# Projections made two chunks at a time: sixteen wide products, then sixteen narrow ones

## The chip, the cores and the metric

The kernel runs on one core of one Trainium2 chip. The metric is device time in microseconds (us): the time of one execution of the program. Lower is better. The parts of the core that matter here are TensorE (PE in the profile), which multiplies matrices and leaves its sums in PSUM banks; ScalarE (ACT) and VectorE (DVE), which prepare operands and empty those banks; SyncE (SP), which issues the loads of the weights; and GpSimd (POOL), which does little.

## The reference

The reference is an encoder of two layers on an input of 256 tokens with 1024 channels, all in float32. Each layer adds two sub-layers to the stream `h`:

```
u, q, k, v, g_pool, g_attn = split(rmsnorm(x) @ w_in)     # 1024, 3 x 1536, 1024, 1024 columns
pooled  = centred means of u (windows 2, 4, 8, 16 for 4 groups of 256) - u
pool    = (pooled_g @ w_pool_g for each group) * pool_scale
attn    = dilated window attention, 12 heads of 128 in 3 groups of 4,
          with relative-position bias, the groups combined by their softmax sums
merged  = sigmoid(g_pool) * (pool @ w_a) + sigmoid(g_attn) * (attn @ w_b)
x      += merged @ w_o
a, g    = split(rmsnorm(x) @ w_up)                        # 2816 columns each
x      += (gelu(conv3(a) + conv_b) * g) @ w_down
```

A final RMSNorm follows. Nearly all the work is in the products with `w_in`, `w_pool`, `w_a`, `w_b`, `w_o`, `w_up` and `w_down`.

## The kernel before, in words

**How a product keeps its precision.** A float32 matrix is held as two parts, a high one and a low one, in the type fp32r. A weight piece (mostly 1024 input rows by 128 output columns) arrives by a DMA as `raw` (L117); ACT casts it to the high part `wh` (L177), and DVE subtracts that from `raw` to make the low part `wl` (L178). Here this is called a split. The activations are held the same way, side by side: `x2` is [high | low], 256 tokens each, 512 columns wide. A product then has two kinds of step. A wide one multiplies `wh` by all 512 columns of [high | low]; a narrow one multiplies `wl` by the 256 high columns, and adds into the second half of the same bank. The product low by low is left out.

**A projection.** One chunk of 128 output channels is made by `proj` (L489): it takes a weight piece from `W.get`, claims one of the four PSUM banks of the pool `mmp`, and calls `two_sums` (L473), which issues the steps: eight wide (one for each 128 rows of the 1024) and eight narrow. The flag `turns["rest"]` turns over at each call. If one call does the wide steps first, the next does the narrow ones first. So PE's stream is eight wide, then sixteen narrow (eight of this chunk and eight of the next), then sixteen wide, and so on. The chunk is then read by ACT and DVE (an eviction), mostly in `add_up` (L508): ACT copies one half, DVE adds the other to it. Only after that does the bank come free.

**The callers.** In each layer these use `two_sums`:

- the pooling inputs `u` (L811): 8 chunks, one after another; in layer 0 one step of `build_bias` (L367) goes ahead of each, five in all, which puts a pair of small products (`f_ps`, L374) in PE's stream;
- the queries and keys (L962): six groups `PAIRS` of two query chunks and two key chunks, 24 chunks. In the second group (`m == 1`) one step of `pool_out` goes ahead of each of the four chunks;
- `pool_out` (L841): each step makes two chunks of the pooled output, with only two wide and two narrow steps for each (the groups have 256 channels). Below, such a step is called a pool pair, 1 to 4. ACT and DVE scale both (L855 and the line after) and split the result into `po2`;
- from the fourth group on (`m >= 3`), after every second chunk, one step of the attention: scores (`s_ps`, L882), turning (`pt_ps`, L911) or weighing (`o_ps`), on PE's fp32 and fp32r products;
- `pa` (L987): 8 chunks of `po2 @ w_a`, most of them followed by an attention step;
- the gates (L995): 16 chunks, 8 for the pooled branch and then 4 and 4 for the attention branch, each 4 followed by four chunks `b_ps` of `at2 @ w_b`, with four wide and four narrow steps each (L1012);
- the MLP (L1085): for each of 22 blocks `f` a chunk `g` and, from `f = 4` on, a chunk `a`. From `f = 6` on, after every two blocks, two rows of the product with `w_down` follow (`residual_mm`, L512 to L514), three products for each output tile.

The values `v`, the products with `w_o` and `w_down` and the first four `a` chunks are made in other ways and do not use `two_sums`.

**What sets the order.** The program is written in one order, and each engine works through its own queue in that order. Work that depends on another engine's waits for it by semaphores, which the tile framework places. Splits are asked for three pieces ahead (`LOOK = 3`); there are three `raw` buffers and five pairs of `wh` and `wl` (`RAW` and `BUFS`, L84). `W.get` issues the splits that are due before the products that use the piece, so on ACT and DVE they stand between the evictions of earlier chunks. PSUM has eight banks: four in `mmp`, four in `acc` (sums of `residual_mm`, scores and others).

Of the kernel before, what the change touches and what calls it, by code (L numbers as in the profile page):

```python
# [10 lines left out]
F32 = mybir.dt.float32  # L11
# [5 lines left out]
P = 128  # L17
D = 1024
S = 256
# [185 lines left out]
def encoder(ctx, tc, x, w_in, w_pool, pool_scale, w_a, w_b, w_o, norm1, norm2, w_up, conv_w,  # L205
# [264 lines left out]

    turns = {"rest": False}

    def two_sums(ps, wh, wl, x2, nk):  # L473

        steps = [(k, True) for k in range(nk)]
        rests = [(k, False) for k in range(nk)]  # L480
        steps = rests + steps if turns["rest"] else steps + rests
        for n, (k, wide) in enumerate(steps):
            out, w, x = (ps, wh, x2[:, k]) if wide else (ps[:, 1], wl, x2[:, k, 0])
            nc.tensor.matmul(  # L484
                out, w(k), x, start=(n == 0), stop=(n == 2 * nk - 1), skip_group_check=turns["rest"]
            )
        turns["rest"] = not turns["rest"]

    def proj(x2):  # L489

        i, (wh, wl) = W.get()
        ps = mmp.tile([P, 2, S], F32, tag="mm", name="proj_ps")
        two_sums(ps, lambda k: wh[:, k, :], lambda k: wl[:, k, :], x2, KD)
        W.free(i)
        return ps[:, 0], ps[:, 1]

    def halves(a):

# [2 lines left out]
    def in_order(a):  # L501

        return a.rearrange("p (m t) -> p t m", t=2)
# [248 lines left out]
    for l in range(DEPTH):  # L752
# [50 lines left out]
        for gi in range(3, -1, -1):  # L803
            w = WINDOWS[gi]
            u = sm.tile([P, 2, S + 2 * PAD], F32, tag="u", name="u")
            nc.vector.memset(u[:, :, 0:PAD], 0.0)
            nc.vector.memset(u[:, :, PAD + S :], 0.0)
            for j in range(2):
                if l == 0:
                    next(bias, None)  # L810
                add_up(in_order(u[:, j, PAD : PAD + S]), [halves(a) for a in proj(x2)])  # L811
            cur, n = u, S + 2 * PAD
            sh = 1
            while sh < w:
                nxt = sm.tile([P, 2, S + 2 * PAD], F32, tag="us", name="us")
                n -= sh
                nc.vector.tensor_add(
                    out=nxt[:, :, 0:n], in0=cur[:, :, 0:n], in1=cur[:, :, sh : sh + n]
                )
                cur = nxt  # L820
                sh *= 2
            hw = w // 2
            o = PAD - hw
            e = edge[:, gi, 0:hw].unsqueeze(1).to_broadcast([P, 2, hw])
            nc.vector.tensor_mul(out=cur[:, :, o : o + hw], in0=cur[:, :, o : o + hw], in1=e)
            if hw > 1:
                e = edge[:, gi, hw : w - 1].unsqueeze(1).to_broadcast([P, 2, hw - 1])
                r = slice(o + S - hw + 1, o + S)
                nc.vector.tensor_mul(out=cur[:, :, r], in0=cur[:, :, r], in1=e)
            pd = sm.tile([P, 2, S], F32, tag="us", name="pd")  # L830
            nc.vector.scalar_tensor_tensor(
                out=pd, in0=cur[:, :, o : o + S], scalar=1.0 / w, in1=u[:, :, PAD : PAD + S],
                op0=ALU.mult, op1=ALU.subtract,
            )
            both = pl2[gi // 2][:, gi % 2 * 2 : gi % 2 * 2 + 2]
            ph, pl = both[:, :, 0], both[:, :, 1]
            pd = pd.rearrange("p k (m t) -> p k t m", t=2)
            nc.scalar.copy(out=ph, in_=pd)
            nc.vector.tensor_sub(out=pl, in0=pd, in1=ph.bitcast(F32))
            pooled[gi] = both  # L840
        def pool_out(po2):  # L841
            for j in range(2):
                i, (wh, wl) = W.get()
                for gg in range(2):
                    for oc in range(2):
                        ps = mmp.tile([P, 2, S], F32, tag="mm", name="pool_ps")
                        cc = slice(oc * P, (oc + 1) * P)
                        two_sums(
                            ps, lambda k: wh[:, 2 * gg + k, cc], lambda k: wl[:, 2 * gg + k, cc],
                            pooled[2 * j + gg], 2,  # L850
                        )
                        c = 4 * j + 2 * gg + oc
                        sc = hps[:, l, c : c + 1]
                        po = sm.tile([P, 2, P], F32, tag="u", name="po")
                        nc.scalar.mul(out=po, in_=halves(ps[:, 1]), mul=sc)  # L855
                        nc.vector.scalar_tensor_tensor(
                            out=po, in0=halves(ps[:, 0]), scalar=sc, in1=po, op0=ALU.mult, op1=ALU.add
                        )
                        nc.scalar.copy(out=po2[:, c, 0], in_=po)
                        nc.vector.tensor_sub(out=po2[:, c, 1], in0=po, in1=po2[:, c, 0].bitcast(F32))  # L860
                    if gg:
                        W.free(i)
                    yield
# [87 lines left out]
        for m, c in enumerate(PAIRS):  # L951
            if m == 1:
                po2 = two_parts("m2", "po2")
                pool_parts = pool_out(po2)
            if m == 2:

                qkl = big.tile([P, 2, HPG, 2, P], F32R, tag="xn", name="qkl")
                ql, kl = qkl[:, 0], qkl[:, 1]
            for n in range(4):
                if m == 1:  # L960
                    next(pool_parts)
                src, rest = (halves(a) for a in proj(x2))  # L962
                hd = 2 * c + n % 2
                scale = HD**-0.5 if n < 2 else 1.0
                if hd < HPG:
                    hi, lo = ((qh, ql) if n < 2 else (kh, kl))
                    nc.scalar.mul(out=hi[:, hd], in_=src, mul=scale)
                    nc.vector.scalar_tensor_tensor(
                        out=lo[:, hd], in0=src, scalar=scale, in1=hi[:, hd].bitcast(F32),
                        op0=ALU.mult, op1=ALU.subtract,  # L970
                    )
                    nc.vector.scalar_tensor_tensor(
                        out=lo[:, hd], in0=rest, scalar=scale, in1=lo[:, hd].bitcast(F32),
                        op0=ALU.mult, op1=ALU.add,
                    )
                else:
                    o = (q if n < 2 else kk)[:, hd - HPG]
                    nc.scalar.mul(out=o, in_=rest, mul=scale)
                    nc.vector.scalar_tensor_tensor(
                        out=o, in0=src, scalar=scale, in1=o, op0=ALU.mult, op1=ALU.add  # L980
                    )
                if m >= 3 and n % 2:
                    step()
# [10 lines left out]

        def gate(c):  # L995
            th = gates[:, c % 4, :]
            add_up(th, proj(x2))
            nc.scalar.activation(th, th, AF.Tanh, scale=0.5)  # L998
            return th

# [7 lines left out]
        for c4 in range(2):  # L1008
            ths = [gate(4 * c4 + j) for j in range(4)]
            for j2 in range(2):  # L1010
                i, (wh, wl) = W.get()
                for j in range(2):  # L1012
                    c = 4 * c4 + 2 * j2 + j
                    ps = mmp.tile([P, 2, S], F32, tag="mm", name="b_ps")
                    cc = slice(j * P, (j + 1) * P)
                    two_sums(ps, lambda k: wh[:, k, cc], lambda k: wl[:, k, cc], at2, 4)
                    m = sm.tile([P, S], F32, tag="u", name="m")
                    add_up(m, (ps[:, 0], ps[:, 1]))
                    nc.vector.scalar_tensor_tensor(
                        out=m, in0=ths[2 * j2 + j], scalar=1.0, in1=m, op0=ALU.add, op1=ALU.mult  # L1020
                    )
                    nc.vector.tensor_add(out=m, in0=m, in1=pa[:, c, :])
                    m = halves(m)
                    nc.scalar.copy(out=mh[:, c], in_=m)
                    nc.vector.tensor_sub(out=ml[:, c], in0=m, in1=mh[:, c].bitcast(F32))
                W.free(i)
# [50 lines left out]
        for i, _ in held:  # L1077
            W.free(i)
        last = keep_entry(ps)
        g_first = [proj(x2)]  # L1080
        turn_entry(1, last)

        def up(f):
            w0, w1, w2, b = (prm[:, l, j * NF + f : j * NF + f + 1] for j in range(4))
            if f < ENTRY:  # L1085
                a = a_first[:, f, :]
            else:
                a = sm.tile([P, S], F32, tag="u", name="a")
                add_up(in_order(a), [halves(b) for b in proj(x2)])
            sums = g_first.pop() if f == 0 else proj(x2)  # L1090
            y = sm.tile([P, S], F32, tag="s", name="y")
            nc.scalar.activation(y, a, AF.Identity, bias=b, scale=w1)  # L1092
            nc.vector.scalar_tensor_tensor(  # L1093
# [85 lines left out]
```

## Time and profile before

| what | before |
| --- | --- |
| median of 3 runs | 880.12 us (879.62 to 880.17) |
| the profiled execution's own time | 880.35 us |
| its span, from the first to the last instruction | 878.6 us |
| mean granted clock of TensorE | 0.998 |
| PE busy | 870.6 us, 99% |
| DVE busy | 684.6 us, 78% |
| ACT busy | 524.3 us, 60% |
| POOL busy | 13.5 us, 2% |
| moved by DMA | 164.47 MB, 187 GB/s |

A row of the timeline gives the start and the length in us, the engine, the line of the kernel, the operation, what it writes and what it reads, the tile's shape, and how many instructions of one kind in a row were put together (x16). A length reaches from the start of the first to the end of the last. Consecutive products overlap on PE, so the time that a run of products takes is read from its start to the start of the next run. A note in brackets is the time that the engine idled ahead of the row, and what it waited for.

### The profile page before, as it was taken

The page shows a single profiled execution, that of the slowest core. Times are in us where ns is not written, and L with a number is a line of the kernel's source. Part 1 is how long each engine was busy: PE and PEld are TensorE (multiplying, and loading weights), DVE is VectorE, ACT ScalarE, POOL GpSimd, SP SyncE. Part 2 cuts the span into 40 slices and gives each one's busy share as a digit, 9 for nine tenths or more (in the row PEclk, how much of TensorE's full clock was granted, in tenths as well). Part 3 has the DMA queues.
Part 4 walks back from the last instruction along what each step waited for, and adds up shares of the span by engine and source line. Part 5 has one row for each costly group of instructions (what it writes and reads, how often), then busy time and mean ns, then how long its engine had stood idle before and what let it go on. Part 6 is the DMA issues. An engine that isn't in the chain of part 4 may idle for free.

```text
span 878.6 us, 12705 instructions
## 1 busy us (share of the span) xinstructions
PE 870.6 (99%) x4817; PEld 757.3 (86%) x4817; DVE 684.6 (78%) x1167; ACT 524.3 (60%) x929; POOL 13.5 (2%) x40
## 2 busy tenths in 40 slices
PE   9999999999999999999999999999999999999996
PEld 7888889988888888888888888899888888888885
DVE  6988886766868987877755987776678698877874
ACT  6745654556647766666545565454666486666662
POOL 2000000000000000000000000000000000000000
PEclk9999999999999999999999999999999999999999
DMA  9669744455565466465636465443556447456431
GB/s 327 230 205 310 248 144 147 143 178 161 190 212 193 145 230 202 144 227 205 240 120 219 163 198 188 149 159 126 190 192 212 151 151 253 169 191 214 170 144 49
DMA packets 125790, 164.47 MB, mean 187 GB/s; under 512 B 2995, under 2 KB 106107, under 8 KB 125600
## 3 DMA queue, kind: packets, MB, share of 16 engines
q1 hardware_dynamic: 125712, 163.65, 55.5%
q8 instruction: 38, 0.62, 0.3%
q14 instruction: 24, 0.20, 0.1%
q10 hardware_dynamic: 16, 0.00, 0.0%
HBM read 162.57 MB, written 3.69 MB: 189 GB/s over the span
## 4 chain that ended last, share of the span: by engine, by line
PE 99%; ACT 0%; POOL 0%; DVE 0%; issue 0%; POOLq 0%; ACTq 0%
PE proj_ps L484 61%; PE v_ps L582 6%; PE res_ps L512 6%; PE res_ps L514 6%; PE res_ps L513 6%; PE b_ps L484 3%; PE v_ps L744 2%; PE v_ps L657 1%; PE pool_ps L484 1%; PE o_ps L932 1%; PE s_ps L882 1%; PE pt_ps L911 1%; PE s_ps L877 1%; PE o_ps L928 1%; PE xt_ps L450 1%; PE gain_ps L333 0%
## 5 line engine op out<-in xcount | busy, mean ns | idle before, releaser
L178 DVE TENSOR_TENSOR wl<-raw,wh 128x1024 fp32r<-128x1024 f32 x274 | 333.9, 1222 | 85.9 <-ACT wh L177 83.6
L484 PE MATMUL proj_ps<-x,wh 128*128 128x512 f32 x1408 | 344.5, 392 | 0.0
L177 ACT CAST wh<-raw 128x1024 fp32r<-128x1024 f32 x274 | 286.5, 1050 | 79.8 <-PE res_ps L514 38.8
L484 PEld LDWEIGHTS proj_ps<-x,wh 128*128 128x128 f32 x1408 | 257.5, 188 | 49.8 <-issue 0.5
L484 PEld LDWEIGHTS proj_ps<-x,wl 128*128 128x128 f32 x1408 | 180.9, 191 | 7.4 <-issue 0.2
L484 PE MATMUL proj_ps<-x,wl 128*128 128x256 f32 x1408 | 184.2, 283 | 0.0
L512 PE MATMUL res_ps<-wh,actq 128*128 128x512 f32 (+1 forms) x184 | 70.0, 380 | 0.0
L513 PE MATMUL res_ps<-wl,actq 128*128 128x512 f32 (+1 forms) x184 | 69.9, 380 | 0.0
L514 PE MATMUL res_ps<-wh,actk 128*128 128x512 f32 (+1 forms) x184 | 69.9, 380 | 0.0
L1092 ACT ACTIVATE y<-a,prm 128x256 f32<-128x256 f32 x36 | 21.6, 601 | 40.5 <-DVE a L508 40.5
L513 PEld LDWEIGHTS res_ps<-wl,actq 128*128 128x128 f32 x184 | 34.6, 188 | 6.6
L512 PEld LDWEIGHTS res_ps<-wh,actq 128*128 128x128 f32 x184 | 34.6, 188 | 6.6
L514 PEld LDWEIGHTS res_ps<-wh,actk 128*128 128x128 f32 x184 | 34.6, 188 | 6.6
L484 PE MATMUL proj_ps<-po,wh 128*128 128x512 f32 x128 | 32.1, 396 | 0.0
L1093 DVE SCALAR_TENSOR_TENSOR y<-a,prm,y 128x255 f32<-128x255 f32 x36 | 17.4, 482 | 14.1 <-ACT y L1092 14.1
L484 PEld LDWEIGHTS proj_ps<-po,wh 128*128 128x128 f32 x128 | 23.1, 189 | 4.2
L512 PE MATMUL res_ps<-wh,m 128*128 128x512 f32 (+1 forms) x72 | 26.5, 368 | 0.0
L514 PE MATMUL res_ps<-wh,m 128*128 128x512 f32 (+1 forms) x72 | 26.3, 365 | 0.0
L513 PE MATMUL res_ps<-wl,m 128*128 128x512 f32 (+1 forms) x72 | 26.3, 365 | 0.0
L416 ACT ACTIVATE junk<-h 128x512 f32<-128x512 f32 (+1 forms) x20 | 10.9, 547 | 25.7 <-DVE h L414 25.7
L582 PE MATMUL v_ps<-wh,x 128*128 128x512 f32 x80 | 25.7, 392 | 0.0
L998 ACT ACTIVATE gates<-gates 128x256 f32<-128x256 f32 x32 | 13.1, 415 | 18.9 <-DVE gates L508 18.9
(208 smaller groups left out, 1104.3 us busy)
## 6 DMA issues: line engine op xcount, KB each, us to landing
raw<-in_w_in_dram SPq DMA_DIRECT2D x58, 1024.0 KB, 6.0
raw<-in_w_up_dram SPq DMA_DIRECT2D x44, 1024.0 KB, 5.0
raw<-in_w_down_dram SPq DMA_DIRECT2D x22, 1024.0 KB, 4.8
raw<-in_w_a_dram SPq DMA_DIRECT2D x8, 1024.0 KB, 4.9
raw<-in_w_o_dram SPq DMA_DIRECT2D x8, 1024.0 KB, 5.2
raw<-in_w_b_dram SPq DMA_DIRECT2D x4, 1024.0 KB
sk<-fd SPq DMA_DIRECT2D x1, 2560.0 KB
raw<-in_w_pool_dram SPq DMA_DIRECT2D x2, 1024.0 KB
```

Of the source, the lines that this page charges most:

```text
L177: lambda: nc.scalar.copy(out=h, in_=src),
L178: lambda: nc.vector.tensor_sub(out=l, in0=src, in1=h.bitcast(F32)),
L416: nc.scalar.activation(junk[:, 0 : cc.stop - cc.start], h[:, t, cc], AF.Square, scale=D**-0.5, accum_out=ss[:, n : n + 1],)
L484: nc.tensor.matmul(out, w(k), x, start=(n == 0), stop=(n == 2 * nk - 1), skip_group_check=turns["rest"])
L512: nc.tensor.matmul(ps, ah, wh, start=first, stop=False)
L513: nc.tensor.matmul(ps, ah, wl, start=False, stop=False)
L514: nc.tensor.matmul(ps, al, wh, start=False, stop=last)
L582: nc.tensor.matmul(ps, x2[:, 2 * n + j, part, t, :], w[:, j, :], start=(n + m == 0), stop=(n == 3 and m == 5),)
L744: nc.tensor.matmul(ps[t], a[:, k, t, :], w[:, j, :], start=(k + m == 0), stop=(k == KD - 1 and m == 2),)
L998: nc.scalar.activation(th, th, AF.Tanh, scale=0.5)
L1092: nc.scalar.activation(y, a, AF.Identity, bias=b, scale=w1)
L1093: nc.vector.scalar_tensor_tensor(out=y[:, 1:], in0=a[:, : S - 1], scalar=w0, in1=y[:, 1:], op0=ALU.mult, op1=ALU.add)
```

## The change

`two_sums` takes several chunks. It issues the first kind of step of all of them, then the other kind of all of them. `proj(x2, n)` makes `n` chunks in one call and hands out one at a time from the list `ready`; the callers' loops stay as they were. It asks for both weight pieces ahead of the products, and claims both banks. The pairs are: two chunks `u` of a group, two query or two key chunks, two gate chunks, two `g` chunks at the MLP's start, and from `f = 4` on the `a` and `g` chunk of one block. The two chunks of a pool pair, and the two `b_ps` chunks that share a weight piece, are paired as well. The chunks `pa` stay single. Each pair turns `turns["rest"]` over once, so PE's stream becomes sixteen wide, then sixteen narrow of the same two chunks, then sixteen narrow of the next two, then sixteen wide.

Where a pair is made in one call, what was issued between its two chunks now stands after both: a step of `build_bias`, a pool pair, the eviction of the first chunk. A pool pair that stood ahead of a second chunk now stands behind that pair.

```
-    def two_sums(ps, wh, wl, x2, nk):
-        steps = [(k, True) for k in range(nk)]
-        rests = [(k, False) for k in range(nk)]
-        steps = rests + steps if turns["rest"] else steps + rests
-        for n, (k, wide) in enumerate(steps):
-            out, w, x = (ps, wh, x2[:, k]) if wide else (ps[:, 1], wl, x2[:, k, 0])
-            nc.tensor.matmul(
-                out, w(k), x, start=(n == 0), stop=(n == 2 * nk - 1), skip_group_check=turns["rest"]
-            )
+    def two_sums(x2, nk, *chunks):
+        wide, rests = ([(c, k, kind) for c in chunks for k in range(nk)] for kind in (True, False))
+        first = rests if turns["rest"] else wide
+        last = wide if turns["rest"] else rests
+        for steps in (first, last):
+            for (ps, wh, wl), k, kind in steps:
+                out, w, x = (ps, wh, x2[:, k]) if kind else (ps[:, 1], wl, x2[:, k, 0])
+                nc.tensor.matmul(
+                    out, w(k), x, start=(steps is first and k == 0),
+                    stop=(steps is last and k == nk - 1), skip_group_check=turns["rest"],
+                )
         turns["rest"] = not turns["rest"]
...
-    def proj(x2):
-        i, (wh, wl) = W.get()
-        ps = mmp.tile([P, 2, S], F32, tag="mm", name="proj_ps")
-        two_sums(ps, lambda k: wh[:, k, :], lambda k: wl[:, k, :], x2, KD)
-        W.free(i)
-        return ps[:, 0], ps[:, 1]
+    def columns(banks, wh, wl, k0=0):
+        return [
+            (
+                ps,
+                lambda k, c=c: wh[:, k0 + k, c * P : (c + 1) * P],
+                lambda k, c=c: wl[:, k0 + k, c * P : (c + 1) * P],
+            )
+            for c, ps in enumerate(banks)
+        ]
+
+    ready = []
+
+    def proj(x2, n=1):
+        if not ready:
+            pieces = [W.get() for _ in range(n)]
+            ps = [mmp.tile([P, 2, S], F32, tag="mm", name="proj_ps") for _ in range(n)]
+            two_sums(
+                x2, KD,
+                *(
+                    (b, lambda k, wh=wh: wh[:, k, :], lambda k, wl=wl: wl[:, k, :])
+                    for b, (_, (wh, wl)) in zip(ps, pieces)
+                ),
+            )
+            for i, _ in pieces:
+                W.free(i)
+            ready.extend((b[:, 0], b[:, 1]) for b in ps)
+        return ready.pop(0)
...
-                add_up(in_order(u[:, j, PAD : PAD + S]), [halves(a) for a in proj(x2)])
+                add_up(in_order(u[:, j, PAD : PAD + S]), [halves(a) for a in proj(x2, 2)])
...
-                    for oc in range(2):
-                        ps = mmp.tile([P, 2, S], F32, tag="mm", name="pool_ps")
-                        cc = slice(oc * P, (oc + 1) * P)
-                        two_sums(
-                            ps, lambda k: wh[:, 2 * gg + k, cc], lambda k: wl[:, 2 * gg + k, cc],
-                            pooled[2 * j + gg], 2,
-                        )
+                    both = [mmp.tile([P, 2, S], F32, tag="mm", name="pool_ps") for _ in range(2)]
+                    two_sums(pooled[2 * j + gg], 2, *columns(both, wh, wl, 2 * gg))
+                    for oc, ps in enumerate(both):
...
-                src, rest = (halves(a) for a in proj(x2))
+                src, rest = (halves(a) for a in proj(x2, 2))
...
-            add_up(th, proj(x2))
+            add_up(th, proj(x2, 2))
...
-                for j in range(2):
+                both = [mmp.tile([P, 2, S], F32, tag="mm", name="b_ps") for _ in range(2)]
+                two_sums(at2, 4, *columns(both, wh, wl))
+                for j, ps in enumerate(both):
...
-        g_first = [proj(x2)]
+        g_first = [proj(x2, 2)]
...
-                add_up(in_order(a), [halves(b) for b in proj(x2)])
-            sums = g_first.pop() if f == 0 else proj(x2)
+                add_up(in_order(a), [halves(b) for b in proj(x2, 2)])
+            sums = g_first.pop() if f == 0 else proj(x2, 2)
```

More of the change, by code (lines that the diff above doesn't have):

```diff
@@ L471, in encoder @@
     turns = {"rest": False}
-    def two_sums(ps, wh, wl, x2, nk):
-        steps = [(k, True) for k in range(nk)]
-        rests = [(k, False) for k in range(nk)]
-        steps = rests + steps if turns["rest"] else steps + rests
-        for n, (k, wide) in enumerate(steps):
-            out, w, x = (ps, wh, x2[:, k]) if wide else (ps[:, 1], wl, x2[:, k, 0])
-            nc.tensor.matmul(
-                out, w(k), x, start=(n == 0), stop=(n == 2 * nk - 1), skip_group_check=turns["rest"]
-            )
-        turns["rest"] = not turns["rest"]
-    def proj(x2):
-        i, (wh, wl) = W.get()
-        ps = mmp.tile([P, 2, S], F32, tag="mm", name="proj_ps")
-        two_sums(ps, lambda k: wh[:, k, :], lambda k: wl[:, k, :], x2, KD)
-        W.free(i)
-        return ps[:, 0], ps[:, 1]
+    def two_sums(x2, nk, *chunks):
[9 more added lines that the diff above has]
+                )
+        turns["rest"] = not turns["rest"]
+    def columns(banks, wh, wl, k0=0):
[4 more added lines that the diff above has]
+                lambda k, c=c: wl[:, k0 + k, c * P : (c + 1) * P],
+            )
+            for c, ps in enumerate(banks)
[16 more added lines that the diff above has]
+        return ready.pop(0)
     def halves(a):
@@ L1011, in encoder @@
                 i, (wh, wl) = W.get()
-                for j in range(2):
+                both = [mmp.tile([P, 2, S], F32, tag="mm", name="b_ps") for _ in range(2)]
+                two_sums(at2, 4, *columns(both, wh, wl))
+                for j, ps in enumerate(both):
                     c = 4 * c4 + 2 * j2 + j
-                    ps = mmp.tile([P, 2, S], F32, tag="mm", name="b_ps")
-                    cc = slice(j * P, (j + 1) * P)
-                    two_sums(ps, lambda k: wh[:, k, cc], lambda k: wl[:, k, cc], at2, 4)
                     m = sm.tile([P, S], F32, tag="u", name="m")
```

## The prediction

> **What bounds the kernel now.** I read the page's busy shares first, then the chain of work that ended last, then the costliest groups, then what PE waited for, and only then the order of single instructions in the timeline.
>
> ```profile
> span 878.6 us, 12705 instructions
> PE 870.6 (99%) x4817; PEld 757.3 (86%) x4817; DVE 684.6 (78%) x1167; ACT 524.3 (60%) x929; POOL 13.5 (2%) x40
> ...
> PE 99%; ACT 0%; POOL 0%; DVE 0%; issue 0%; POOLq 0%; ACTq 0%
> ...
> L178 DVE TENSOR_TENSOR wl<-raw,wh 128x1024 fp32r<-128x1024 f32 x274 | 333.9, 1222 | 85.9 <-ACT wh L177 83.6
> L484 PE MATMUL proj_ps<-x,wh 128*128 128x512 f32 x1408 | 344.5, 392 | 0.0
> L177 ACT CAST wh<-raw 128x1024 fp32r<-128x1024 f32 x274 | 286.5, 1050 | 79.8 <-PE res_ps L514 38.8
> ...
> L484 PE MATMUL proj_ps<-x,wl 128*128 128x256 f32 x1408 | 184.2, 283 | 0.0
> ```
>
> ```profile
> PE gain_ps L333 <- DVE ones L319: 1.0, 1, 1.0
> PE v_ps L657 <- ACT xuh L613: 0.2, 1, 0.2
> ```
>
> PE is the bound from end to end: 99% busy, 99% of the chain, and the two waits that the trace names both lie in the first microseconds. No engine ever holds a projection up. So the change can win only by making PE's own stream shorter, and it can lose only by making PE wait. The durations of 392 and 283 ns overlap and cannot be summed; what a product costs is the distance between starts.
>
> **Part 1: fewer switches between wide and narrow.** The first two rows of the next fence give the distance of wide products in a stretch that has no narrow ones: twelve of them from 403.16 to 405.88, 0.2267 us each. The others show sixteens in turn.
>
> ```profile
> 403.16 0.39 PE L514 MATMUL res_ps<-wh,actk 128*128 128x512 f32 x1
> ...
> 405.88 0.39 PE L514 MATMUL res_ps<-wh,actk 128*128 128x512 f32 x1
> ```
>
> ```profile
> 97.06 2.08 PE L484 MATMUL proj_ps<-x,wl 128*128 128x256 f32 x16
> 98.97 3.82 PE L484 MATMUL proj_ps<-x,wh 128*128 128x512 f32 x16
> 102.62 2.08 PE L484 MATMUL proj_ps<-x,wl 128*128 128x256 f32 x16
> 104.54 3.82 PE L484 MATMUL proj_ps<-x,wh 128*128 128x512 f32 x16
> 108.19 2.08 PE L484 MATMUL proj_ps<-x,wl 128*128 128x256 f32 x16
> ```
>
> Sixteen narrow take 1.91 and 1.92 us, 0.12 each; sixteen wide behind them take 3.65 twice (98.97 to 102.62, 104.54 to 108.19), where sixteen of 0.2267 would take 3.63. So a switch from narrow to wide costs about 0.025 us, and a switch back gives back at most 0.01. Counted in the built order of PE's matmuls, the change takes the switches narrow to wide from 112 to 62 and those back from 128 to 74: about 52 of each go, which at 0.013 to 0.023 net is 0.7 to 1.2 us. I take **-0.95**. The runs of sixteen already cross from one chunk into the next, so a change of bank inside a run costs nothing; runs of 32 exist nowhere here, which the third rival uses.
>
> By the Trainium skill (TensorE: Matmul & The Clock Gate, Back-to-back issue gap) warm matmuls that follow each other start N/2.4 + 2.5 ns apart, about 216 ns for 512 columns and 109 for 256, with no term for the kind of the one before. By that rule this part is worth nothing and the sum below would be 0.95 us higher; the rows disagree with it in level (227 and 120) and in the 3.65.
>
> **Part 2: where the small products cut in.** The order of other PE work moves with the pairs. The five bias pieces (L374) cut into the projections five times; in the new order they come in three groups.
>
> ```profile
> 47.27 2.00 PE L484 MATMUL proj_ps<-x,wh 128*128 128x512 f32 x8
> 49.20 0.28 PE L374 MATMUL f_ps<-onehot_r,rh 33*4 33x256 f32 x1
> 49.32 0.28 PE L374 MATMUL f_ps<-onehot_r,rl 33*4 33x256 f32 x1
> 49.53 2.09 PE L484 MATMUL proj_ps<-x,wh 128*128 128x512 f32 x8
> 51.46 1.11 PE L484 MATMUL proj_ps<-x,wl 128*128 128x256 f32 x8
> 52.50 0.28 PE L374 MATMUL f_ps<-onehot_r,rh 33*4 33x256 f32 x1
> 52.62 0.28 PE L374 MATMUL f_ps<-onehot_r,rl 33*4 33x256 f32 x1
> 52.82 1.22 PE L484 MATMUL proj_ps<-x,wl 128*128 128x256 f32 x8
> 53.87 2.00 PE L484 MATMUL proj_ps<-x,wh 128*128 128x512 f32 x8
> ```
>
> Amid narrow ones a cut costs 0.08 before (51.46 to 52.50 against 8 x 0.12), 0.08 inside (52.50 to 52.82 for two of 0.12) and 0.09 behind (52.82 to 53.87): 0.25; amid wide ones 0.09 + 0.09 + 0.11 = 0.29. Two cuts fewer: **-0.55**.
>
> In the attention steps, small fp32 products (L882, L911) are followed by wide products 8 times less often, and by narrow ones 6 times more often, since pairs end on the other kind.
>
> ```profile
> 113.46 2.09 PE L484 MATMUL proj_ps<-x,wh 128*128 128x512 f32 x8
> 115.39 0.28 PE L484 MATMUL proj_ps<-x,wl 128*128 128x256 f32 x1
> ```
>
> ```profile
> 152.42 1.20 PE L484 MATMUL proj_ps<-po,wl 128*128 128x256 f32 x8
> 153.45 0.86 PE L484 MATMUL proj_ps<-po,wh 128*128 128x512 f32 x3
> ```
>
> Eight wide behind such products take 1.93 (0.12 over), eight narrow 1.03 (0.07 over): -8 x 0.12 + 6 x 0.07 = -0.54; I take **-0.45**, as two of the eight are cuts inside a chunk.
>
> **Part 3: two banks at once.** There are four PSUM banks in mmp. A pair claims two and gives both back late, when ACT and DVE have emptied them. In most stages a pair of whole projections (5.56 us) lies in between, and that covers it. It does not in the pooling projections, where a pool pair lasts 4 x 0.2267 + 4 x 0.12 = 1.39 us and DVE has nothing to spare:
>
> ```profile
> 78.50:97.10 18.60, 18.60 (x106) 16.27 (x105) 18.07 (x31) 15.81 (x30) 0.00 (x0) 1.00 0.90 299
> ```
>
> ```profile
> 77.22 2.95 ACT L177 CAST wh<-raw 128x1024 fp32r<-128x1024 f32 x3 [0.92 <-DMA raw<-in_w_in_dram]
> 78.30 2.36 DVE L178 TENSOR_TENSOR wl<-raw,wh 128x1024 fp32r<-128x1024 f32 x2 [1.55 <-ACT wh L177]
> 78.51 0.61 PE L484 MATMUL pool_ps<-pl,wh 128*128 128x512 f32 x2
> 83.73 0.42 DVE L979 SCALAR_TENSOR_TENSOR q<-proj_ps,q 128x256 f32<-128x256 f32 x1
> 85.04 2.00 PE L484 MATMUL proj_ps<-x,wh 128*128 128x512 f32 x8
> 86.88 0.62 PE L484 MATMUL pool_ps<-pl,wh 128*128 128x512 f32 x2
> 87.08 0.39 ACT L978 ACTIVATE q<-proj_ps 128x256 f32<-128x256 f32 x1 [0.46 <-PE proj_ps L484]
> ```
>
> In the first row the columns are PE, PEld, DVE, ACT and POOL busy: DVE 18.07 of 18.60. From the others: ACT starts on a result 0.20 after PE's next product (86.88 to 87.08); casts follow at 0.95 (three in 2.95); two DVE splits take 2.36; an eviction is 0.39 on ACT and 0.42 on DVE.
>
> Layer 0 in the new order, with pool pair 1 at 78.51 as before: it ends at 79.90, the q pair (narrow first) at 85.48, pool pair 2 at 86.87, the first chunk of pool pair 3 at 87.58. Its second chunk takes the bank of pool pair 2's first chunk, whose DVE eviction stands behind q0's and two splits. q0 is done at 83.67; ACT 83.87 to 84.26, DVE to 84.69; ACT casts two pieces, 84.15 to 86.15; DVE splits them from 85.22 to 87.58; then the eviction, done at 87.95 or so. PE waits **0.4**. Behind the waiting product stand the whole k pair and all after it, for PE takes them in order. The next narrow place, the pair behind pool pair 4, comes out free by 0.2.
>
> Layer 1, from the start of its pool pair 1: pool pair 3 ends at 9.75; the k pair needs the bank of pool pair 2's first chunk. Here DVE's order is q0, split, q1, split, eviction: split 6.70 to 7.90, q1 to 8.27, split 8.50 to 9.72, eviction to 10.10. PE waits **0.4**, and **0.15** for k0's eviction before the next pair. Together the four places give +0.95; I take **+1.0**. Bounds: 0, as everything ends within 0.4 of its need, and 1.0 plus one more split each (1.18), 5.7. I stay low because each step has its duration in a row.
>
> By the Trainium skill (TensorE: Matmul & The Clock Gate, Architectural detail) ACT and DVE work strictly in order, so an eviction cannot pass the split before it. That speaks against the change and is what the two walks assume; in the rows DVE's starts keep the built order.
>
> **Part 4: the rest costs nothing.** Products, splits, evictions and DMAs are as many as before. SP's queue keeps its order of loads, each waiting for a split that moves by less than a pair; the loads that the pool stage waits for (0.92 in the row at 77.22) stand behind bias copies that become ready a little earlier. POOL is untouched. The start of the MLP, where no w_down rows lie between the pairs, is the next tightest.
>
> ```profile
> 283.50 0.41 DVE L508 TENSOR_TENSOR g<-proj_ps,g 128x256 f32<-128x256 f32 x1
> ...
> 288.38 2.08 PE L484 MATMUL proj_ps<-x,wl 128*128 128x256 f32 x16
> ```
>
> The fourth g is evicted by 283.91, and its bank is needed in the second half of the narrow run at 288.38. The new order needs that bank 1.8 us earlier and evicts it 3 later: some 0.6 stay. If that cover is gone, it costs up to one split, 1.2, in each layer.
>
> **Sum.** -0.95 - 0.55 - 0.45 + 1.0 = -0.95 us. The profiled execution took 880.35 and goes to 879.4; the median of the runs shown is 880.12, 0.23 below it, so I forecast **879.2**.
>
> **Rivals.** First, slower: the banks decide. If at the four places of Part 3 one more split stands ahead, the waits are 5.7 and the sum is +3.75: 883.9. For it: DVE at 97%. Against it: that order of splits is the built one, already counted. It makes the kernel slower by over 0.2% (1.76 us, about what can be told from no change here) once the waits pass 3.7 us. Second, faster: DVE gets there in time, waits 0, -1.95: 878.2. For it: margins of a few tenths. Third, the switch costs nothing that pairing saves, or a run of 32 narrow products makes the next wide ones dearer by as much: 880.1, no change.
>
> **How the numbers follow.** The forecast has 0.5, slower 0.2, faster 0.2, the third 0.1. The forecast and the third lie within 0.2%, as does a small part of the two others' weight; so faster 0.2, same 0.6, slower 0.2. The forecast's own range is 878.2 to 880.6 (waits of 0 to 2.4). For 8 in 10 I go down to 877.8 (1.2 for the switches and no wait) and up to 882.6, part of the way to the first rival.
>
> **What would show it.** Right: wide sixteens become 32 and take 16 x 0.2267 more; three bias groups; PE waits on DVE, a few tenths each, at pool_ps or the pair behind it, and nowhere else. Wrong: waits of over 1 us at the pool stage, any wait in the MLP or at b_ps, or wide runs that lose more than 0.03 behind 32 narrow ones.

## The result, and the profile after

| | before | after |
| --- | --- | --- |
| median | 880.06 us (8 runs, 879.62 to 880.46) | 882.31 us (8 runs, 881.18 to 884.01) |
| profiled execution | 880.35 us, span 878.6 | 882.09 us, span 880.3 |

The ratio is 1.0025, with a 95% interval of 1.0015 to 1.0034. The change makes the kernel slower by about 0.25%. The forecast was 879.2 us, a little faster. The measured time lies in the wider range that was given (8 chances in 10, 877.8 to 882.6), near its upper end, but outside the forecast's own (878.2 to 880.6) and on the other side of the time before. The runs also spread more: 2.8 us against 0.8.

The page of the changed kernel, its head and its chain of waits:

```profile
span 880.3 us, 12693 instructions
PE 869.5 (99%) x4817; PEld 756.6 (86%) x4817; DVE 681.2 (77%) x1167; ACT 530.7 (60%) x929; POOL 13.1 (1%) x40
...
PE 93%; DMA 3%; DVE 2%; ACT 1%; issue 0%; SPq 0%; POOL 0%; ACTq 0%; POOLq 0%
```

PE is busy for 1.1 us less than before, and yet the span is 1.7 us longer. The chain is no longer PE alone: DMA, DVE and ACT now have 6% of it. What PE waited for (total, times, longest):

```profile
PE pool_ps L486 <- DVE po L879: 1.4, 1, 1.4
...
PE xt_ps L450 <- DVE xn L441: 0.6, 1, 0.6
...
PE proj_ps L486 <- DVE po L879: 0.3, 1, 0.3
...
PE proj_ps L486 <- DVE wl L178: 0.2, 1, 0.2
```

All four are new, and lie in three places. The first is the pooled stage of layer 0 (timeline of the changed kernel):

```profile
78.13 0.63 PE L486 MATMUL pool_ps<-pl,wl 128*128 128x256 f32 x4
...
78.95 1.21 PE L486 MATMUL proj_ps<-x,wl 128*128 128x256 f32 x8 [0.19 <-DVE wl L178]
...
80.00 0.40 PE L486 MATMUL proj_ps<-x,wh 128*128 128x512 f32 x1
...
80.42 1.22 PE L486 MATMUL proj_ps<-x,wl 128*128 128x256 f32 x8
...
84.69 2.00 ACT L177 CAST wh<-raw 128x1024 fp32r<-128x1024 f32 x2 [1.02 <-DMA raw<-in_w_in_dram]
...
85.78 2.36 DVE L178 TENSOR_TENSOR wl<-raw,wh 128x1024 fp32r<-128x1024 f32 x2 [1.65 <-ACT wh L177]
...
86.53 0.63 PE L486 MATMUL pool_ps<-pl,wh 128*128 128x512 f32 x2
...
88.06 0.87 DVE L879 SCALAR_TENSOR_TENSOR po<-pool_ps,hps,po 128x256 f32<-128x256 f32 x2
...
88.59 0.50 PE L486 MATMUL pool_ps<-pl,wl 128*128 128x256 f32 x2 [1.43 <-DVE po L879]
...
88.93 0.63 PE L486 MATMUL pool_ps<-pl,wh 128*128 128x512 f32 x2
```

The two wide products at 86.53 should end in PE's order by 86.98 (2 x 0.2267), and the next starts at 88.59: 1.61 us of waiting, and 0.10 more behind it (two narrow take 0.34 instead of 0.24). PE needs a bank whose eviction stands on DVE at 88.06, behind two splits, as the prediction said. The splits are late because ACT's casts at 84.69 waited 1.02 us for a load, which the prediction did not say. In the same way, 78.13 to 78.95, 80.00 to 80.42 and the runs behind them lose 0.43 and 0.29. In all the stage costs 2.4 us.

PE's order in these rows is not quite the paired one of the text above: the pair of projections is eight narrow, one wide, eight narrow, fifteen wide, and the third pool pair is made one chunk after the other. So the order that was built, in which an engine works, is not always the one in which the program is written. In layer 1 the same pairs are built as written (16 and 16, 8 and 4).

The second is the end of layer 0's MLP. First the changed kernel's timeline, then that of before:

```profile
421.22 13.23 SPq L117 DMA_DIRECT2D raw<-in_w_in_dram  x5
...
435.68 1.06 ACT L177 CAST wh<-raw 128x1024 fp32r<-128x1024 f32 x1 [0.20 <-DMA raw<-in_w_in_dram]
...
436.77 1.23 DVE L178 TENSOR_TENSOR wl<-raw,wh 128x1024 fp32r<-128x1024 f32 x1 [2.11 <-ACT wh L177]
...
437.91 0.69 DVE L414 TENSOR_TENSOR h<-res_ps,h 128x512 f32<-128x512 f32 x1
...
438.69 0.63 ACT L416 ACTIVATE junk<-h 128x512 f32<-128x512 f32 x1 [1.95 <-DVE h L414]
...
440.24 0.28 PE L541 MATMUL res_ps<-wh,actk 128*128 128x256 f32 x1
...
441.07 0.74 PE L450 MATMUL xt_ps<-ident,xn 128*128 128x128 f32 x4 [0.55 <-DVE xn L441]
...
441.57 0.37 PE L539 MATMUL res_ps<-wh,actq 128*128 128x256 f32 x1
```

```profile
418.06 15.38 SPq L117 DMA_DIRECT2D raw<-in_w_in_dram  x5
...
433.44 1.05 ACT L177 CAST wh<-raw 128x1024 fp32r<-128x1024 f32 x1 [1.83 <-DMA raw<-in_w_in_dram]
...
436.58 0.63 ACT L416 ACTIVATE junk<-h 128x512 f32<-128x512 f32 x1 [1.46 <-DVE h L414]
```

The loads for the next layer's values begin at 421.22 instead of 418.06, so the cast is at 435.68 instead of 433.44. DVE has the split of that piece (436.77) ahead of its part of the norm (`h`, L414, 437.91; before, 434.53 and 435.80), so the squares (`junk`, L416) move from 436.58 to 438.69, and PE waits for the normed rows: 0.71 from 440.24 to 441.07 beyond the usual 0.12, and 0.15 in the four transposes behind it.

The third is the pooled stage of layer 1:

```profile
518.98 1.23 DVE L178 TENSOR_TENSOR wl<-raw,wh 128x1024 fp32r<-128x1024 f32 x1 [0.25 <-ACT wh L177]
...
519.29 1.09 PE L486 MATMUL pool_ps<-pl,wh 128*128 128x512 f32 x4
...
520.13 0.87 DVE L879 SCALAR_TENSOR_TENSOR po<-pool_ps,hps,po 128x256 f32<-128x256 f32 x2
...
520.66 3.94 PE L486 MATMUL proj_ps<-x,wh 128*128 128x512 f32 x16 [0.27 <-DVE po L879]
...
526.82 1.09 PE L486 MATMUL pool_ps<-pl,wh 128*128 128x512 f32 x4
...
527.87 2.37 PE L486 MATMUL proj_ps<-x,wh 128*128 128x512 f32 x9
```

Four wide take 0.91, and here 1.37 and 1.05 pass: 0.46 and 0.14; with the slow first steps behind them it is 0.8. (From 510.48, its first pool step, to 531.67 the stage takes 21.19 us; in the kernel below that makes it unpaired, the same work takes 20.36.)

One more difference is not the change's. The start of the kernel, before any projection, took 0.7 us less in this execution. The first row is of before, the second of after (in the kernel with both of the edits told of below it starts at 7.70):

```profile
8.52 0.73 PE L657 MATMUL v_ps<-m,xuh 128*128 128x512 f32 x2 [0.22 <-ACT xuh L613]
```

```profile
7.82 0.73 PE L684 MATMUL v_ps<-m,xuh 128*128 128x512 f32 x2 [0.22 <-ACT xuh L640]
```

It varies by as much without the change: the same row starts at 8.41 and at 7.83 in two other kernels of the old order, the one without the bias copies and the one without the turn. So the account is: span +1.7 = start -0.7, waits +2.4 + 0.9 + 0.8 = +4.1, and the rest -1.7, which is put down to what the pairs save; an experiment below checks it.

### The profile page after: what moved, and what is told of

It reads as the page before. It is cut to its first block, busy times and chain, and to the rows that moved or that the text cites. A ratio compares the mean times of both kernels' runs of the same rounds, so it can differ in the third digit from the quotient of the medians.

```text
span 880.3 us, 12693 instructions
## 1 busy us (share of the span) xinstructions
PE 869.5 (99%) x4817; PEld 756.6 (86%) x4817; DVE 681.2 (77%) x1167; ACT 530.7 (60%) x929; POOL 13.1 (1%) x40
## 4 chain that ended last, share of the span: by engine, by line
PE 93%; DMA 3%; DVE 2%; ACT 1%; issue 0%; SPq 0%; POOL 0%; ACTq 0%; POOLq 0%
PE proj_ps L486 57%; PE v_ps L609 6%; PE res_ps L539 6%; PE res_ps L541 6%; PE res_ps L540 6%; PE b_ps L486 3%; PE v_ps L771 2%; DMA raw<-in_w_in_dram 1%; PE v_ps L684 1%; DMA sk<-fd 1%; PE o_ps L955 1%; PE s_ps L905 1%; PE pt_ps L934 1%; PE s_ps L900 1%; PE o_ps L951 1%; PE xt_ps L450 1%
## 5 line engine op out<-in xcount | busy, mean ns | idle before, releaser
L486 PE MATMUL proj_ps<-x,wh 128*128 128x512 f32 x1408 | 334.2, 391 | 0.3 <-DVE po L879 0.3
L486 PEld LDWEIGHTS proj_ps<-x,wh 128*128 128x128 f32 x1408 | 260.7, 188 | 53.5 <-DVE po L879 0.7
L486 PEld LDWEIGHTS proj_ps<-x,wl 128*128 128x128 f32 x1408 | 175.4, 191 | 4.4 <-DVE wl L178 0.4
L486 PE MATMUL proj_ps<-x,wl 128*128 128x256 f32 x1408 | 178.6, 283 | 0.2 <-DVE wl L178 0.2
L1127 ACT ACTIVATE y<-y 128x256 f32<-128x256 f32 x44 | 18.4, 419 | 41.4 <-DVE y L1118 41.3
L416 ACT ACTIVATE junk<-h 128x512 f32<-128x512 f32 (+1 forms) x20 | 10.9, 547 | 25.3 <-DVE h L414 25.2
L534 ACT COPY gates<-proj_ps 128x256 f32<-128x256 f32 x32 | 11.9, 373 | 23.4 <-PE proj_ps L486 23.4
```

What stands on the lines that cost most here:

```text
L416: nc.scalar.activation(junk[:, 0 : cc.stop - cc.start], h[:, t, cc], AF.Square, scale=D**-0.5, accum_out=ss[:, n : n + 1],)
L486: nc.tensor.matmul(out, w(k), x, start=(steps is first and k == 0), stop=(steps is last and k == nk - 1), skip_group_check=turns["rest"],)
L534: nc.scalar.copy(out=out, in_=sums[1])
L1127: nc.scalar.activation(y2, y, AF.Square, scale=float(np.sqrt(0.044715)))
```

## The experiments

Two questions: what makes PE wait at each of the three places, and whether the saving is there. Theory A: a pair holds banks until DVE empties them, and in layer 0 DVE is late because the weight loads stand behind the bias copies. Theory C: at the end of the MLP a pair holds its weight buffers longer, so loads start later. The rivals are in the expectations.

**The pooled stage unpaired.** In the second group of queries and keys, chunks and pooled outputs one at a time:

```
-                src, rest = (halves(a) for a in proj(x2, 2))
+                src, rest = (halves(a) for a in proj(x2, 1 if m == 1 else 2))
...
-                    both = [mmp.tile([P, 2, S], F32, tag="mm", name="pool_ps") for _ in range(2)]
-                    two_sums(pooled[2 * j + gg], 2, *columns(both, wh, wl, 2 * gg))
-                    for oc, ps in enumerate(both):
+                    for oc in range(2):
+                        ps = mmp.tile([P, 2, S], F32, tag="mm", name="pool_ps")
+                        one = columns([ps, ps], wh, wl, 2 * gg)[oc]
+                        two_sums(pooled[2 * j + gg], 2, one)
```

> The changed kernel, but in the second group of queries and keys (m == 1) the chunks and the pooled outputs are made one at a time, in both layers, as before. Theory A (a pair holds two of four banks, and in layer 0 the weight loads behind the bias copies come late for the splits that stand ahead of the evictions): PE's waits in that stage, 2.4 us in layer 0 and 0.8 in layer 1, go; four more switches cost 0.1; the wait of 0.9 at the end of layer 0's MLP stays: 882.3 - 3.2 + 0.1 = 879.2 us. Rival B (in layer 0 PE waits for the loads themselves, since it now reaches them 1.3 us earlier, whatever the order of the chunks): only layer 1's 0.8 goes, 881.6 us.

Measured: 879.17 us (12 runs), 0.9988 of before (0.9980 to 0.9996). No wait is left in either pooled stage; the one at the MLP's end is there (0.5 in the waits). Theory A's number came out; rival B, that PE waits for the loads in any order, fell: PE begins the stage of layer 0 as early as in the changed kernel (77.11 against 77.22) and does not wait.

**The last two blocks unpaired.**

```
-                add_up(in_order(a), [halves(b) for b in proj(x2, 2)])
-            sums = g_first.pop() if f == 0 else proj(x2, 2)
+                add_up(in_order(a), [halves(b) for b in proj(x2, 1 if f >= NF - 2 else 2)])
+            sums = g_first.pop() if f == 0 else proj(x2, 1 if f >= NF - 2 else 2)
```

> The changed kernel, but the last two blocks of the MLP (f = 20 and 21) make a and g one at a time. Theory C (a pair gives its weight buffers back later, so the loads for the next layer start 3 us later, and DVE, which splits them in order, is late for the norm): the wait of 0.9 us at the end of layer 0's MLP goes, two more switches cost under 0.1: 881.4 us, and the load that started at 421.2 us starts at about 418.7. Rival D (that wait was one late load by chance): the start of the load moves little, the wait is there or not in either kernel, and the median stays at 882.3 us.

Measured: 880.37 us (12 runs, 879.41 to 883.51), 1.0002 of before (0.9992 to 1.0012). The timeline of this kernel at the place:

```profile
419.44 15.52 SPq L117 DMA_DIRECT2D raw<-in_w_in_dram  x5
...
420.65 0.39 PE L539 MATMUL res_ps<-wh,actq 128*128 128x512 f32 x1
...
441.12 0.60 PE L450 MATMUL xt_ps<-ident,xn 128*128 128x128 f32 x4
```

The first load starts 1.21 us ahead of PE's row of `w_down` (420.65), as it did before (418.06 against 419.28); in pairs it started 1.34 behind it (421.22 against 419.88). So the pair moved the load by 2.6 us against PE, and without it the wait is gone: rival D fell. That the pair does it is shown; that it does so by its weight buffers is in part argued. With the blocks single, the cast whose split frees that load's buffer waited 0.18 us for PE to be done with a weight buffer (417.10). In pairs it stands at 418.89, behind the eviction of the pair's first chunk (418.27), which had waited for PE as well, and no run separates the two. The gain in the median, 1.9 us from 882.3, is twice the 0.9 expected from one trace, and that stays open: PE's wait there is 0.5 to 0.6 in all six traces that keep the pair and the queue, and in the kernel of the first edit the same change takes away 1.1 (879.17 to 878.05, below). This trace is of an execution of 882.01 us, 1.6 above the median.

**Both.**

> Both edits together: pairs everywhere but in the pooled stage and the last two blocks of the MLP. Theories A and C: no wait is left on PE, only the saving of fewer switches and cuts: 880.1 - 1.6 = 878.5 us, below the kernel before. Rivals B and D: waits of 2 to 3 us are left, 880.5 to 881.5 us. If the saving itself isn't there (pairs save no time on PE): 880.1 us with no waits.

Measured: 878.05 us (9 runs, 877.85 to 878.80), 0.9974 of before (0.9964 to 0.9983). PE's waits are those of the start:

```profile
PE gain_ps L333 <- DVE ones L319: 1.0, 1, 1.0
PE v_ps L684 <- ACT m L185: 0.4, 1, 0.4
PE v_ps L684 <- ACT xuh L640: 0.2, 1, 0.2
```

The span is 876.1 us: 2.5 less than before, 0.8 of it in the start (8.52 to 7.70), so the pairs save 1.7 on PE where they are left. The saving is real, and the spread of the runs is small again. This version is faster than both kernels.

**The turn taken away**, in the kernel before, to price a switch by adding many:

```
-        turns["rest"] = not turns["rest"]
```

> The kernel before, without the turn: each chunk makes its wide products first, so PE's order has 82 more switches from narrow to wide and 100 more back, 6 more wide runs and 8 fewer narrow ones behind the attention's small products. By the prediction's prices (0.025 us a switch to wide, 0.008 given back, 0.117 and 0.073 behind small products): +2.05 - 0.8 + 0.1 = +1.4, 881.5 us. If a switch has no price, as the rule of the Trainium skill on the gap between products has it: 880.2 us.

Measured: 881.61 us (10 runs), 1.0017 of before (1.0008 to 1.0026), with no new wait; by the prediction's prices it was to be 881.5. The MLP of layer 0 shows the price alone. The rows are the first product of `w_down` at the start of the first and of the eighth group of four chunks, in the kernels before, after and without the turn:

```profile
303.26 0.39 PE L512 MATMUL res_ps<-wh,actq 128*128 128x512 f32 x1
...
419.28 0.39 PE L512 MATMUL res_ps<-wh,actq 128*128 128x512 f32 x1
```

```profile
304.01 0.39 PE L539 MATMUL res_ps<-wh,actq 128*128 128x512 f32 x1
...
419.88 0.39 PE L539 MATMUL res_ps<-wh,actq 128*128 128x512 f32 x1
```

```profile
303.14 0.40 PE L511 MATMUL res_ps<-wh,actq 128*128 128x512 f32 x1
...
419.43 0.40 PE L511 MATMUL res_ps<-wh,actq 128*128 128x512 f32 x1
```

Seven groups take 116.02, 115.87 and 116.29 us: 0.021 less for each group with one switch there and back fewer, 0.039 more for each with two more. A switch there and back costs 0.02 us, whichever way it is changed. The rule of the Trainium skill (TensorE: Matmul & The Clock Gate, Back-to-back issue gap) has no such term, and these rows disagree with it. That section of the Trainium skill gives its formula for an isolated product, and for a stream about 131 ns at 512 columns; the 0.2267 us of the prediction's rows is above both.

**The changed kernel again**, unedited.

> The changed kernel itself, unedited, to have its waits in a second trace and its time beside those of the next three. Theory A: the wait at the pooled stage of layer 0 follows the landing of the load that SP issues behind the bias copies (issued 76.6 us, landed 84.6 us, PE resumed at 88.6 us in the first trace; 77.8, 85.4 and 89.4 us in the kernel with single blocks at the end): PE resumes 4.0 us after that landing again, and layer 1's waits stay at 0.4 and 0.1. Rival B2 (banks and DVE's order alone): the wait is the same in each execution. Median 881 to 882.5 us.

Measured: 882.23 us (11 runs, 880.52 to 883.28), 1.0014 of before (1.0005 to 1.0023). The chain of waits at the pooled stage of layer 0 in three kernels, the load (start, time to landing) and PE's resuming: the changed kernel's first trace, this one, and the kernel with the last blocks unpaired, which is the same there.

```profile
76.62 8.00 DMA raw<-in_w_in_dram
...
88.59 0.97 PE pool_ps L486 x4
```

```profile
78.23 6.93 DMA raw<-in_w_in_dram
...
89.13 0.97 PE pool_ps L486 x4
```

```profile
77.75 7.63 DMA raw<-in_w_in_dram
...
89.35 0.97 PE pool_ps L486 x4
```

The loads land at 84.62, 85.16 and 85.38, and PE resumes 3.97 us behind each. PE's wait there is 1.61, 1.42 and 2.14 us, so it is as long as the load is late for PE; rival B2 fell. A landing that varies also fits the spread of the runs, which is small where nothing waits for it (0.95 us with both edits).

**Without the bias copies.** Both kernels, with `bt` filled with zeros, so that the attention's bias is left out:

```
-        sk = dram.tile([P, n + 1], F32, name="sk")
-        nc.sync.dma_start(out=sk[:, 0:n], in_=fd[0].partition_broadcast(P))
-        for blk, kind in enumerate((2, 0, 1, 3, 4)):
...
-            nc.sync.dma_start(out=bt[:, :, blk * P : (blk + 1) * P], in_=src)
+        nc.gpsimd.memset(bt, 0.0)
```

> The changed kernel without the copies that lay out the attention's bias (sk and bt; bt is filled with zeros instead, so the attention's bias is left out). Theory A: the loads land in time, PE's wait at the pooled stage of layer 0 falls from about 2.4 us to what layer 1 has (0.4 to 0.8), the wait at the MLP's end stays: 882.3 - 1.8 = 880.5 us. Rival B2 (banks and DVE's order alone, the loads don't matter): 882.3 us, with the wait of 1.6 us in place.

> The kernel before without those copies (bt filled with zeros, the attention's bias left out). Theory A: PE had no wait there, so nothing is gained: 880.1 us, within 0.3. If the copies slow PE in some other way (its operands, its clock), it is faster by as much as the changed kernel is.

Measured: the changed kernel 880.75 us (10 runs), 1.0002 of before; the kernel before 880.33 us (10 runs), 0.9996 of itself with the copies (0.9986 to 1.0005). The copies cost the old order nothing and the new one 1.5 us. Layer 0 without them (timeline):

```profile
87.46 2.80 PE L480 MATMUL proj_ps<-x,wh 128*128 128x512 f32 x11 [0.27 <-DVE po L873]
```

That wait, 0.27 for DVE's `po`, is the one that layer 1 has at 520.66. From its first pool step (77.28) to the 32 narrow products behind it (98.47) layer 0's stage now takes 21.19 us, as layer 1's did; with the copies it took 22.79, and unpaired 20.36. So layer 0's 2.4 us is made of the bank wait, which both layers have (0.8), and of late loads (1.6). One thing differs besides the copies: without them layer 0's pairs are built as they are written. What that alone changes is not separated, but the three traces above, with one built order, show the loads' part by themselves.

**The copies into `bt` on another queue.**

```
-            nc.sync.dma_start(out=bt[:, :, blk * P : (blk + 1) * P], in_=src)
+            nc.gpsimd.dma_start(out=bt[:, :, blk * P : (blk + 1) * P], in_=src)
```

> The changed kernel with the five copies into bt issued on POOL's queue, so that on SP's queue no weight load stands behind them; the copy into sk stays. Theory A with the order of SP's queue as the cause: the load that was issued at 76.6 us is issued as soon as a raw buffer is free, before 74 us, lands before 82 us, and layer 0's wait falls to 0.4 to 0.8: 880.6 us. If the cause is the copies' share of the DMA engines (2.6 MB into sk until 72 us) and not the queue: the load lands about as late as before, and the time stays near 882 us.

Measured: 882.88 us (9 runs), 1.0026 of before (1.0016 to 1.0035): nothing won. In the trace the load did start earlier, and the longest wait of the pooled stage went from 1.4 to 0.3, but the one at the MLP's end was longer:

```profile
PE xt_ps L450 <- DVE xn L441: 1.5, 1, 1.5
...
PE proj_ps L486 <- DVE po L879: 0.6, 2, 0.3
```

The load at fault was issued at the same place in this kernel and in the changed one, 10.59 us behind the first product of that group of `w_down`, and took 6.11 us to land (from 429.69) in place of 5.13 (from 430.47). That queue and the unpaired last blocks were put together:

> The changed kernel with the copies into bt on POOL's queue and the last two blocks of the MLP one at a time. With the copies moved alone the median was 882.9 us, though the wait at layer 0's pooled stage had shrunk to layer 1's size; its trace had a longer wait at the MLP's end, 1.7 us in place of 0.9. If the loss of that kernel lies there, the single blocks take it away: 881.2 us or less. If the move to POOL's queue costs elsewhere, 882 us or more.

Measured: 880.78 us (11 runs), 1.0011 of before (1.0002 to 1.0020). By the expectation the loss lay at the MLP's end. But single blocks win as much on the old queue (1.9 us; here 2.1), so the runs show neither a gain nor a loss by the new queue: 0.6 us more with pairs at the end and 0.4 more without, both within the noise. In the traces layer 0's stage is a little shorter for it, 22.00 against 22.79 us with pairs at the end and 23.07 against 23.54 without, far from the 20.36 of the unpaired one. The chain of this kernel has the load that the copies into `bt` no longer stand ahead of:

```profile
69.71 13.80 DMA raw<-in_w_in_dram
```

Issued at 69.71, it lands at 83.5. The copies, issued from 73.7 to 76.9, now run beside the load instead of standing ahead of it. That fits the Trainium skill (DMA: Bandwidth & Descriptors, Queues, rings and completion order), by which each DMA engine takes packets from its queues in turn. It is not shown, though: the load issued before it on its own queue (64.03) was on its way until about 77 too, as the cast at 77.50 waited for it. Why the load at the MLP's end took longer with the new queue alone stays open.

**One half of the pooled stage at a time.** First only the queries and keys single (the first line of the first edit), then only the pooled outputs (the rest of it):

> The changed kernel, but the queries and keys of the second group (m == 1) one at a time; the pooled outputs stay in pairs. If what costs time in that stage is that pairing the projections puts pool pairs 2 and 3 next to each other, with 1.39 us of products each between a bank's claim and its next: the projections stand between them again, the waits at the pooled stage go in both layers, the wait at the MLP's end stays: 879.2 us. If it is that a pool pair claims two banks at once: the waits stay, 882 us.

> The other half: the pooled outputs one chunk at a time, the queries and keys of the second group in pairs. By the first reading the waits stay, as pool steps 2 and 3 are still next to each other: 882 us, with 0.4 and 0.1 us in layer 1. By the second they go: 879.2 us.

Measured: 879.99 us (10 runs), 0.9995 of before (0.9986 to 1.0005), and 881.01 us (10 runs, 879.47 to 883.64), 1.0012 (1.0003 to 1.0021). With the queries and keys single no wait for a bank is left; PE waits 0.4 once in layer 0 for a split, and at the MLP's end. With the pooled outputs single, layer 1 has no wait, and layer 0 waits 0.6 and 0.4 for evictions. So neither reading holds alone: in layer 1 the wait needs both, pool steps next to each other and two banks claimed at once; in layer 0, where loads are late, steps next to each other are enough.

## Why the prediction was wrong

**Part 1, the switches: right.** -0.95 was forecast for some 50 of them; at 0.02 each it is -1.0. The third rival, that runs of 32 give it back, fell with the same rows: a group with a run of 32 narrow products in it is shorter, not as long.

**Part 2, the small products: right in kind, 0.2 to 0.3 too large.** From the first bias piece to the first pool step, the kernel with both edits takes 33.73 us against 34.31: -0.58, where -0.55 was forecast for the cuts; three switches fewer, some 0.06, are in it. All savings together are 1.7, and 1.95 was forecast. 0.1 of the gap is six switches that this version has more than the full change. The rest, 0.1 to 0.2, I put down to the attention steps, which I had priced at 0.117 for a wide run, from one run of eight; no run shows them alone.

**Part 3, the banks in layer 1: right.** The order (split, second query, split, eviction) and the size (0.4 and 0.15 forecast, 0.46 and 0.14 measured) are as walked. Left out was that the run behind each wait starts slowly, 0.12 and 0.15. The Trainium skill's rule that DVE works strictly in order (TensorE: Matmul & The Clock Gate, Architectural detail) agrees: the eviction at 520.13 follows the split of 518.98.

**Part 3, the banks in layer 0: wrong.** The step that failed is "ACT casts two pieces, 84.15 to 86.15". It started the casts when buffers came free and took the load for landed. It landed at 84.62, the casts were at 84.69 to 86.69, and PE had come 0.6 us earlier than in the walk. The forecast was 0.4; 1.7 was measured there, and 0.7 more at the first pair. The sign was to be had: the row quoted for DVE's 18.07 of 18.60 us shows a DMA share of 0.90 in its last columns. Two windows of before (PE, PEld, DVE, ACT, POOL busy, clock, DMA share, GB/s) tell the layers apart:

```profile
64.00:100.00 36.00, 36.00 (x212) 31.88 (x211) 31.96 (x56) 23.55 (x43) 0.00 (x0) 1.00 0.93 293
500.00:540.00 40.00, 40.00 (x235) 35.41 (x234) 33.26 (x53) 25.30 (x46) 0.00 (x0) 1.00 0.65 211
```

Layer 0's stage has its DMA engines 93% busy, layer 1's 65%. A PE that gets there earlier, in an order that needs a bank behind those splits, waits as long as the load is late; in the unpaired order it got there as early and did not wait.

**Part 4, the rest: wrong.** "SP's queue keeps its order of loads, each waiting for a split that moves by less than a pair" is true, and was costed at nothing. A split moved by 2.6 us, less than a pair's 5.56, and the loads for the next layer moved with it. I had searched the MLP's start, where banks are tight, and not its end, where loads are. It cost 0.9 in the trace. The start of the MLP and `b_ps` had no wait, as forecast.

**The sum.** -1.95 + 1.0 was forecast; -1.7 + 4.1 came. The first rival named the right outcome (slower once the waits pass 3.7 us) by a partly wrong mechanism: it had one more split ahead of DVE at four places, and what stood ahead was late loads at two.

## What to carry to other kernels

A pair gives back later what it holds: its PSUM banks and, as it seems here, its weight buffers, and so the loads that need them start later. Before a reordering is costed at nothing, list every stage where a load lands just in time (a cast that waited for DMA, a window with a high DMA share, as 0.93 against 0.65 here), and walk those with the loads' landings, not with the buffers' release. A small saving along the whole kernel is worth having where the slack is, and the few places without it can be left as they were: here that was worth 2 us.

## What was not expected

- A load of 1 MB lands 13.8 us after its issue while the bias copies and the load before it run, as in the row at 69.71. The load at 78.23, behind the copies on one queue, took half as long (6.93).
- After a wait, the first products of the next run are about 0.1 us slower in total: 16 wide in 3.77 us (520.66 to 524.43) against 3.65.
- Moving copies off the queue of the loads won nothing in the time: the load started 8 us earlier (69.71 against 77.75 in the kernel with the last blocks single) and took 6 us longer (13.80 against 7.63), so it landed less than 2 us earlier.
